# Forty projection heads and the block inverses of a DeltaNet layer: order from a scheduler, or from a list in the kernel

## The chip, the cores and the metric

The kernel runs on one core of a Trainium2 chip. The metric is the device time of one launch in microseconds; three runs of the kernel before took 1217.75, 1218.33 and 1227.18 us, the median is 1218.33 us. The profile is of a further execution. Engines are named as in the profile: PE (matmul), PEld (its weight loads), DVE, ACT, POOL, and SP, which here only issues transfers.

## The reference, cut to what matters

Two layers work on 512 latent tokens and 256 context tokens of width 1024, in float32. Layer 0 is a bidirectional gated DeltaNet, layer 1 is attention. The change is in layer 0 alone:

```python
p = u @ w_in                                    # 1024 -> 8192 + 64
qkv = silu(centred_dwconv(p[..., :4096], conv_w))   # five taps per channel
z = p[..., 4096:6144]
q, k, v = split(qkv)        # 8 heads of q, 8 of k, 16 of v, each of 128
...
decay = exp(where(lower, gc[..., :, None] - gc[..., None, :], -inf))
a = where(strict, einsum('cd,sd->cs', kb, kc) * decay, 0)
t_inv = triangular_solve(eye + a, eye)          # per chunk of 64, per head, per direction
qk = einsum('cd,sd->cs', qc, kc) * decay
...
o, s = scan over the chunks with t_inv, qk, k, q, v, in both directions
y = (rms_norm(o) * silu(z)) @ w_out
```

## The kernel before, in words

All 768 tokens lie as 6 tiles of 128 (NT = 6); a tile pairs a chunk of 64 that the forward scan visits with the chunk that the backward scan visits at the same time. Products are float32 made of three passes: an operand is split into a rounded part (wh, uh) and a rest (wl, ul), and wh·uh, wh·ul and wl·uh add up in one PSUM bank.

The program has five stages: conditioning and the transposed input (uh, ul); the projection of 8 key heads (`k_head`); the projection of 8 query heads, 16 gate heads and 16 value heads, beside which the block inverses are made; the scan over the chunks; output projection and the attention layer. The change is in the third stage, from 166.9 to 601.9 us of the profile.

One of its 40 heads is: a 512 KB load of 128 weight columns (SP, tile w, 2 buffers), the rounding to wh (ACT) and the rest wl (DVE; for query heads POOL; 3 buffers each), 24 matmuls of 512 columns into one PSUM bank and 24 of 256 into another (`gemm_T`, L349; 4 banks in all, tag g), and what follows. For query and value heads that is the centre tap (ACT, L368), four taps (DVE, L371), a tanh that is written back into the bank (ACT, L374) and the product that makes SiLU (DVE, L376 or L382), which frees the bank. Query heads are then squared and summed by PE (L504) and stored (q_d); value heads are turned by PE (`to_tokens`, L397), copied by ACT (L768) and stored (v_d) from ACT's queue. Gate heads need only tanh and one product (L778, L779) and a store (z_d).

The block inverses of tile t are made of 32x32 blocks. `t_masked` loads keys (kk) and two sheets of decay rows (df, each 4 broadcast transfers of 128 KB), takes Gram matrices on PE (G, L604), masks them, turns each df into decays by 16 small activations and one exponential (ACT, `decay_of`), and multiplies: md, and mo in four products of 32 partitions each. md is turned (DVE) and weighted (POOL) into L. `t_solve` solves two tiles at a time by columns on POOL (31 pairs of instructions, L682 and L683). `t_join` turns the inverse (U, DVE), takes two sets of 64 block products on PE (pp, L704, and pw, L716) with a negation on ACT between (pn), copies all into Tt (ACT, L708 and L719) and stores t_d. `t_queries` makes the masked products of queries and keys (qk_d) in the same way; their product with df is on POOL.

What sets the order: `pieces` is a generator that yields after each of these parts. The loop over the heads takes them in the order q x8, z x5, (v v z) x8, z z z, splits the weights three heads ahead (`split_ahead`), and after a query, gate or value head takes 1, 3 or 2 parts, which may not be issued before that head's last matmul and the SiLU of the head before (`issue_after`). Within these limits a scheduler of the tile framework, which simulates the program when it is built, places each instruction in its engine's queue. Each engine runs its queue in order. The scan's first loads (`load_step`: cT, cv, cQK, ckt, then ck and cq of the next step) come from the same SP queue.

Of the kernel before, what the change touches and what calls it, by code (L numbers as in the profile page):

```python
# [86 lines left out]
def backbone(tc, a, out):  # L87
# [56 lines left out]
    ul = up.tile([P, KT, NTOK], F32R, tag="ul", name="ul")  # L144

# [176 lines left out]
    split_at = [None, None]  # L322

    def load_w(src, c0, m, nm, E=V):
# [5 lines left out]
        split_at[1] = S.copy(wh[:, :, :m], w[:, :, :m]).ins  # L330
        split_at[0] = E.tensor_tensor(wl[:, :, :m], w[:, :, :m], wh[:, :, :m], ALU.subtract).ins  # L331
        return wh, wl

    tails, at, done = [], [0, None], []

    def turn_tails(age):

        while tails and tails[0][0] <= at[0] - age:
            with tc.issue_after(at[1]):
                tails.pop(0)[1]()  # L340

    def gemm_T(wh, wl, m, nm):

        out_ = []
        for c0, n in ((NCTX, NLAT), (0, NCTX)):
            pg_ = pa.tile([P, 512], F32, tag="g", name=f"g{n}_{nm}", bufs=4)
            for k in range(KT):
                for n_, (w, u) in enumerate(((wh, uh), (wh, ul), (wl, uh))):
                    mm = T.matmul(pg_[:m, :n], w[:, k, :m], u[:, k, c0:c0 + n], start=k == 0 and n_ == 0, stop=k == KT - 1 and n_ == 2)  # L349
            out_.append(pg_)  # L350
            at[1] = mm.ins
            turn_tails(2)
        return out_[1], out_[0]

    split = {}

    def split_ahead(ct, nm, E):

        split[ct] = load_w(w_in, ct * P, P, nm, E)

    def conv_silu(ct, nm, E=V, pool=None, bufs=2, swap=None):

        wh, wl = split.pop(ct) if ct in split else load_w(w_in, ct * P, P, nm, E)
# [9 lines left out]
        for ps, c0, n in ((p5, NCTX, NLAT), (p2, 0, NCTX)):  # L373
            e0 = S.activation(ps[:, :n], acc[:, c0:c0 + n], AF.Tanh)  # L374
            if swap is None:
                e1 = V.scalar_tensor_tensor(s[:, c0:c0 + n], ps[:, :n], 1.0, acc[:, c0:c0 + n], ALU.add, ALU.mult)  # L376
                continue
            h_ = n // 2
            for a0, o0, st_ in ((0, swap * 64, P), (h_, n - P + 64 - swap * 64, -P)):
                dst = raw(s, c0 + o0, [[st_, h_ // 64], [1, 64]])  # L380
                src = [y.rearrange("p (c r) -> p c r", r=64) for y in (ps[:, a0:a0 + h_], acc[:, c0 + a0:c0 + a0 + h_])]
                e1 = V.scalar_tensor_tensor(dst, src[0], 1.0, src[1], ALU.add, ALU.mult)  # L382
        done.append((e0.ins, e1.ins))
# [102 lines left out]
    for b in range(4):  # L486
        for v in range(2):
            r0 = b * 32 + v * 16
            dma(bball[r0:r0 + 16], be_d[v ^ (b // 2)].rearrange("t h c -> h t c")[:, :, b * 32:b * 32 + 32])
# [41 lines left out]
    def q_head(hh):  # L531
# [269 lines left out]
    for _ in work:  # L801
        pass
# [1013 lines left out]
```

## Time and profile before

| | |
|---|---|
| median of 3 runs | 1218.33 us |
| the profiled execution | 1220.96 us, its span 1219.2 us |
| PE busy in the span | 1144.4 us, 94% |
| DVE, ACT, POOL busy | 800.2, 731.5, 579.1 us |
| third stage | 166.9 to 601.9 us |
| mean granted clock of PE in the span | 0.978 |

The span runs from the first to the last instruction on the core; launch and end lie around it (1.8 us here). Matmuls are pipelined and their ends are modelled, so that PE's busy time over many matmuls says when it had work, not how fast it went; how fast is read from the distance between the starts. Busy times of other engines can be added.

### The profile page before, as it was taken

What the parts mean: (1) busy time and instruction counts of PE and PEld (TensorE: products, weight loads), DVE (VectorE), ACT (ScalarE), POOL (GpSimd) and SP (SyncE); (2) the same over time, 40 slices, a digit from 0 to 9 for tenths busy, and PEclk for the clock granted to TensorE, in tenths of its full rate; (3) what the DMA queues carried; (4) which work ended last, traced back from release to release, by engine and by line L of the source; (5) the groups of instructions that cost most, each with busy time, mean ns of one, the idle gap of its engine ahead of it and who ended that gap; (6) DMA issues with size and microseconds to landing.
All of it is one profiled execution on the core that took longest, in us unless ns stands there. A gap on an engine that the chain in (4) does not pass through costs nothing. (4 is left out here: it accounts for less than half of the span.)

```text
span 1219.2 us, 27757 instructions
## 1 busy us (share of the span) xinstructions
PE 1144.4 (94%) x10739; PEld 928.9 (76%) x10739; DVE 800.2 (66%) x1734; ACT 731.5 (60%) x1945; POOL 579.1 (47%) x442
## 2 busy tenths in 40 slices
PE   4999999999789989899999999899999999999996
PEld 1677678888678877788856666688887889999884
DVE  2688565777879645675478888635556566566646
ACT  3344336675565678896268999686663236666731
POOL 0131114229999999830067568455753344230810
PEclk9999899999899998899999999999999999999998
DMA  9465986454436569752999999266672202101323
GB/s 335 137 227 169 338 258 191 130 166 155 132 111 178 162 187 280 235 177 98 295 267 242 260 270 250 76 223 190 217 233 98 70 26 80 52 19 53 104 69 87
DMA packets 171125, 208.73 MB, mean 171 GB/s; under 512 B 12497, under 2 KB 126322, under 8 KB 170226
## 3 DMA queue, kind: packets, MB, share of 16 engines
q1 hardware_dynamic: 151346, 197.02, 53.8%
q10 hardware_dynamic: 19648, 9.94, 2.9%
q8 instruction: 85, 1.39, 0.5%
q14 instruction: 46, 0.38, 0.1%
HBM read 166.16 MB, written 40.67 MB: 170 GB/s over the span
## 5 line engine op out<-in xcount | busy, mean ns | idle before, releaser
L918 POOL TENSOR_TENSOR S<-S,glb 128x512 f32<-128x512 f32 x80 | 81.7, 1043 | 122.0 <-PE ks L909 122.0
L1076 PE MATMUL po<-woh,y 128*128 128x512 f32 x384 | 130.0, 403 | 0.7 <-ACT y L1052 0.7
L349 PE MATMUL g_v<-uh,wh 128*128 128x512 f32 (+1 forms) x256 | 91.4, 357 | 14.8 <-DVE sil_v L376 14.8
L1025 POOL TENSOR_TENSOR wol<-wo,woh 128x1024 fp32r<-128x1024 f32 x32 | 77.1, 2411 | 55.6 <-ACT woh L1018 52.7
L683 POOL TENSOR_TENSOR X<-X,tmp 128x62 f32<-128x62 f32 (+15 forms) x93 | 95.8, 1031 | 6.5
L371 DVE SCALAR_TENSOR_TENSOR acc_v<-g_v,cwv,acc_v 128x510 f32<-128x510 f32 (+3 forms) x128 | 74.5, 610 | 33.9 <-ACT acc_v L368 32.3
L349 PE MATMUL g_z<-uh,wh 128*128 128x512 f32 (+1 forms) x256 | 88.6, 346 | 5.7 <-DVE sil_v L376 5.7
L682 POOL TENSOR_TENSOR tmp<-L,X 128x62 f32<-128x62 f32 (+15 forms) x93 | 89.0, 957 | 6.9
L349 PE MATMUL g_v<-ul,wh 128*128 128x512 f32 (+1 forms) x256 | 89.6, 350 | 0.0
L349 PE MATMUL g_v<-uh,wl 128*128 128x512 f32 (+1 forms) x256 | 88.7, 346 | 0.0
L349 PE MATMUL g_z<-ul,wh 128*128 128x512 f32 (+1 forms) x256 | 87.3, 341 | 0.0
L349 PE MATMUL g_z<-uh,wl 128*128 128x512 f32 (+1 forms) x256 | 87.1, 340 | 0.0
L1076 PEld LDWEIGHTS po<-woh,y 128*128 128x128 f32 x384 | 72.5, 189 | 16.0 <-ACT y L1052 0.9
L1076 PE MATMUL po<-wol,y 128*128 128x512 f32 x192 | 75.7, 395 | 0.9 <-POOL wol L1025 0.9
L349 PEld LDWEIGHTS g_v<-uh,wh 128*128 128x128 f32 x256 | 50.6, 198 | 21.6 <-DVE sil_v L376 15.5
L331 POOL TENSOR_TENSOR wl_k<-w_k,wh_k 128x1024 fp32r<-128x1024 f32 x8 | 19.3, 2415 | 94.6 <-ACT wh_k L330 94.6
L331 POOL TENSOR_TENSOR wl<-w,wh 128x1024 fp32r<-128x1024 f32 x8 | 19.4, 2426 | 83.6 <-ACT wh L330 83.6
L349 PEld LDWEIGHTS g_z<-uh,wh 128*128 128x128 f32 x256 | 49.2, 192 | 11.6 <-DVE sil_v L376 6.4
L331 DVE TENSOR_TENSOR wl<-w,wh 128x1024 fp32r<-128x1024 f32 x32 | 49.9, 1560 | 11.6 <-ACT wh L330 11.6
L1050 DVE SCALAR_TENSOR_TENSOR pt<-pt,og,z 128x128 f32<-128x128 f32 x96 | 34.4, 358 | 34.7 <-PE pt L1041 31.9
L909 PE MATMUL ks<-S,ck 128*64 128x256 f32 x352 | 55.2, 392 | 0.4 <-ACT o L915 0.4
L983 DVE TENSOR_TENSOR S<-su,S 128x512 f32<-128x512 f32 x80 | 51.5, 686 | 6.0 <-PE su L969 3.9
(375 smaller groups left out, 3397.4 us busy)
## 6 DMA issues: line engine op xcount, KB each, us to landing
aw<-in_ada_w SPq DMA_DIRECT2D x24, 1024.0 KB, 7.3
w<-in_dn_w_in SPq DMA_DIRECT2D x40, 512.0 KB, 4.6
wo<-in_dn_w_out SPq DMA_DIRECT2D x32, 512.0 KB, 3.3
cv<-v_d SPq DMA_DIRECT2D x48, 256.0 KB, 8.0
df<-gc_d SPq DMA_DIRECT2D x48, 128.0 KB, 2.8
z_d<-zs SPq DMA_DIRECT2D x16, 384.0 KB, 5.8
v_d<-vt ACTq DMA_DIRECT2D x16, 384.0 KB, 4.0
t_d<-Tt SPq DMA_DIRECT2D x6, 1024.0 KB, 5.1
```

Source lines behind the costliest of these rows:

```text
L331: split_at[0] = E.tensor_tensor(wl[:, :, :m], w[:, :, :m], wh[:, :, :m], ALU.subtract).ins
L349: mm = T.matmul(pg_[:m, :n], w[:, k, :m], u[:, k, c0:c0 + n], start=k == 0 and n_ == 0, stop=k == KT - 1 and n_ == 2)
L371: V.scalar_tensor_tensor(acc[:, c0 + lo:c0 + hi], ps[:, lo + j - 2:hi + j - 2], cwv[:, j, ct:ct + 1], acc[:, c0 + lo:c0 + hi], ALU.mult, A ...
L682: E.tensor_tensor(tv, bcast(L[:, :, j + 1:, j], 3, j + 1), bcast(X[:, :, j, 0:j + 1], 2, n), ALU.mult)
L683: E.tensor_tensor(X[:, :, j + 1:, 0:j + 1], X[:, :, j + 1:, 0:j + 1], tv, ALU.subtract)
L909: T.matmul(ks[r0:r0 + 64, w], kq[w][:, hh, r0:r0 + 64], St[hh][:, d], start=True, stop=True)
L918: G.tensor_tensor(St[hh], St[hh], bcast(g_, 3, P), ALU.mult)
L983: V.tensor_tensor(St[hh], sj, St[hh], ALU.add)
L1025: G.tensor_tensor(wl, raws.pop(n), halves[n][0], ALU.subtract)
L1050: V.scalar_tensor_tensor(pj, pj, og, raw(z, off, [[st_, 2], [1, 64]]), ALU.mult, ALU.mult)
L1076: T.matmul(acc[:, nh], y[i][:, j, :], ww[k][:, nh * 512:(nh + 1) * 512], start=h == 0 and x == 0, stop=h == VH - 1 and x == 2)
```

## The change

The generators, `split_ahead`, `issue_after` and the loop over the heads are gone. All work of the third stage is written as some 750 pieces, each with an engine, a cost in microseconds, a due time, the pieces that it must follow, the buffers that it takes and holds and, for a transfer, a time to land. A greedy pass (`written_out`) goes through them when the program is built: it takes the piece that could start first by these costs, and among equals the one with the earlier due time. The order so found is fixed for all five engines (`manual_schedule`). The costs serve only for the order.

The order of heads becomes z q x8, then v v z x8. A head's bank work is cut into its two parts (512 and 256 columns). The rest wl of query heads moves from POOL to DVE. The weights of a head may be loaded as soon as a buffer is free. The numbers of buffers change: 4 for df in place of 2 (and a borrowed md), Tt has one in place of two. The decay rows are laid out by `lane`, so that all blocks of mo come from the first of the two sheets; mo becomes one product of 128 partitions. The scan and everything behind it are the same.

```diff
+    def lane(b, d):
+        return d ^ (1 - b % 2)
...
+    gcM = ap_.tile(W6, F32, tag="gcM", name="gcM", bufs=1)
+    for b in range(4):
+        for v in range(2):
+            V.tensor_copy(gcM[b * 32:b * 32 + 32, v], gc[b * 32:b * 32 + 32, lane(b, v)])
...
-                decayed(V, md[:, v], df[:, :, 0:32], Gx[:, :, 0:32])
-                for b in ((1, 2), (0, 3))[v]:
-                    r = slice(b * 32, b * 32 + 32)
-                    decayed(V, mo[r], df[r, :, 32:64], Gx[r, :, 32:64])
+        decayed(V, mds[t][:, v], df[:, :, 0:32], Gx[:, :, 0:32])
+        if v == 0:
+            decayed(V, mos[t], df[:, :, 32:64], Gx[:, :, 32:64])
...
-    order = "z" * 5 + "vvz" * 8 + "zzz"
-    heads = [(q_head, h) for h in range(QH)]
...
-        f_(h)
-        with tc.issue_after(split_at[0]), tc.issue_after(split_at[1]), tc.issue_after(at[1]), tc.issue_after(done[-2][0]), tc.issue_after(done[-2][1]):
-            for _ in range({q_head: 1, z_head: 3, v_head: 2}[f_]):
-                next(work, None)
+    order = "zqzqzqzqzqzqzqzqvvzvvzvvzvvzvvzvvzvvzvvz"
...
+    def ready_at(x):
+        at = x.since
+        for y in x.after:
+            if y.end is None:
+                return None
+            at = max(at, y.end + (y.lands if y.engine != x.engine or y.engine == "SP" else 0.0))
...
+        return at + margin(x)
...
+    for n, (c, h) in enumerate(heads):
+        t0 = n * SLOT
+        w = kept(("w", n), Piece("SP", 0.4, t0 - 30, w_load, n, takes=["w"], lands=6.0, since=-99.0))
+        wh = kept(("wh", n), Piece("ACT", 1.05, t0 - 9, w_high, n, after=[w], takes=["wh"], holds=[("w", w)], lands=0.1))
+        G_ = n in ()
+        wl = Piece("POOL" if G_ else "DVE", 2.4 if G_ else 1.5, t0 - 5, w_low, n, G if G_ else V, after=[wh], holds=[("w", w)], lands=0.1)
+        g = []
+        for i in range(2):
+            g.append(Piece("PE", (5.5, 2.9)[i], t0, gemm_part, n, i, after=[wh, wl] + ([last["g", n - 1]] if n and not i else g), takes=["g"], holds=[("wh", wh)], lands=0.2))
...
+    written_p = tc.manual_schedule(engines={T.engine, V.engine, S.engine, G.engine, nc.sync.engine})
+    written_p.__enter__()
+    for _, x in written_out():
+        x.fn()
+    written_p.__exit__(None, None, None)
```

Two places of the program show what moves. The first is the start of the stage. SP's queue before, where the last key head's store (kt7) is issued; w_4 and w_5 are the weights of the fifth and sixth query head:

```order
L329 DMA w_4_2016<-in_dn_w_in 128x8x128
L241 DMA gate_d1_79<-gt100_1603 128x512
L235 DMA gb11_1748<-in_ada_b 128x512
L519 DMA kt_d_65<-kt7_1717 128x6x128
L329 DMA w_5_2138<-in_dn_w_in 128x8x128
L241 DMA gate_d1_79<-gt101_1752 128x512
```

and the same place of SP's queue now; w_z1 and w_q1 are the weights of the third and fourth head of the stage, df0_0m and df1_0m the decay rows of tile 0:

```order
L505 DMA kt_d_65<-kt7_1726 128x6x128
L245 DMA gate_d1_79<-gt101_1761 128x512
L553 DMA df0_0m_1779<-gc_d_69 32x1024 x4
L553 DMA df1_0m_1784<-gc_d_69 32x1024 x4
L723 DMA w_z1_1803<-in_dn_w_in 128x8x128
L723 DMA w_q1_1836<-in_dn_w_in 128x8x128
```

Before, the weights of five heads are asked for ahead of the stores of the last key head; now those of two are, and the third head's come behind these stores and behind the first decay rows. ACT's queue at that place, before; wh_4 is the rounding for the fifth head, and df0_0 are the decays of tile 0:

```order
L526 COPY kb7_1721<-kb1_7_1728 128x2x2x64
L368 ACTIVATE acc_q1_1942<-g512_q1_1892,cwv_74 128x512
L529 DMA k_d_63<-kb7_1721 128x6x128
L534 COPY rq_94<-ss_q0_1857 128x6
L330 CAST wh_4_2017<-w_4_2016 128x1024
```

and now, where the rounding for the third head, wh_z1, stands behind the first sheet of decays:

```order
L515 DMA k_d_63<-kb7_1730 128x6x128
L566 ACTIVATE df0_0m_1779<-df0_0m_1779,gcM_513 128x64 x16
L568 ACTIVATE df0_0m_1779<-df0_0m_1779 128x1024
L566 ACTIVATE df1_0m_1784<-df1_0m_1784,gcM_513 128x64 x6
L765 ACTIVATE sil_z0_1879<-g512_z0_1805 128x512
L728 CAST wh_z1_1881<-w_z1_1803 128x1024
```

ACT now takes 23 instructions on the decays and one on the first gate head before it rounds the weights of the third head. The second place is the end of the stage. SP's queue before; t_d is written from Tt0 and Tt1, elX, cT_0, cv_0, cQK_0 and ckt_0 are the loads of the scan's first step, ck_1 of its second:

```order
L720 DMA t_d_71<-Tt1_1760 128x2048
L781 DMA z_d_68<-zs12_6858 128x768
L850 DMA elX_7097<-elV_90 64x192 x2
L873 DMA cT_0_7106<-t_d_71 128x1024
L878 DMA cv_0_7107<-v_d0_66 64x1024 x2
L881 DMA cQK_0_7108<-qk_d_72 128x4x128
L883 DMA cQK_0_7108<-qk_d_72 64x4x128 x2
L884 DMA ckt_0_7109<-kt_d_65 128x1024
L872 DMA ck_1_7214<-k_d_63 128x1024
L872 DMA cq_1_7215<-q_d_64 128x1024
L781 DMA z_d_68<-zs13_6932 128x768
```

and now:

```order
L815 DMA z_d_68<-sil_z14_6518 128x768
L670 DMA t_d_71<-Tt_1768 128x2048
L815 DMA z_d_68<-sil_z15_6948 128x768
L670 DMA t_d_71<-Tt_1768 128x2048
L1036 DMA elX_7080<-elV_90 64x192 x2
L1059 DMA cT_0_7089<-t_d_71 128x1024
L1064 DMA cv_0_7090<-v_d0_66 64x1024 x2
L1064 DMA cv_0_7090<-v_d1_67 64x1024 x2
L1067 DMA cQK_0_7091<-qk_d_72 128x4x128
L1069 DMA cQK_0_7091<-qk_d_72 64x4x128 x2
L1070 DMA ckt_0_7092<-kt_d_65 128x1024
```

Before, the loads of the scan's first step stand ahead of the stores of the last three gate heads; now all of them stand behind the store of the last gate head (z15) and behind the last store of t_d. On PE the last head's matmuls are now followed by pp and pw of tile 5 and the turn of value head 15, and then by the scan's first product; before, pp and pw of tile 5 and all turns stood ahead of the last two or more gate heads.

More of the change, by code (lines that the diff above doesn't have):

```diff
@@ L800, in backbone, with q_gram @@
[L800 to L805 removed]
+    def q_gram(t):
+        grams[t] = []
+        for gq, kq in enumerate(kks.pop(t)):
+            ps = pa.tile([P, 4, P], F32, tag="gq", name=f"GQ{gq}_{t}")
+            for h4 in range(4):
+                for hf in range(2):
+                    r0 = hf * 64
+                    T.matmul(ps[r0:r0 + 64, h4, 0:64], kq[:, 0, h4, r0:r0 + 64], kq[:, 1, h4, r0:r0 + 64], start=True, stop=True)
+            grams[t].append(ps)
@@ new lines, in head_squared, with head_summed @@
+    def head_squared(n):
+        sums[n] = ap_.tile([P, NT, P], F32, tag="tok", name=f"sq_q{heads[n][1]}").rearrange("p t k -> p (t k)")
+        S.activation(sums[n], sils[n], AF.Square)
+    def head_summed(n):
+        ps = turns[n] = pa.tile([P, 512], F32, tag="tr", name=f"ss_q{heads[n][1]}")
+        sq = sums.pop(n)
+        for t in range(NT):
+            for hf in range(2):
+                c0 = t * P + hf * 64
+                T.matmul(ps[hf * 64:hf * 64 + 64, t:t + 1], sq[:, c0:c0 + 64], ones, start=True, stop=True)
```

550 lines of the change are left out of this document (330 added, 220 removed).

## The prediction

> **What bounds the kernel now.** I read the page first. The busy line shows PE at work nearly all the time, the clock line next to full:
>
> ```profile
> PE 1144.4 (94%) x10739; PEld 928.9 (76%) x10739; DVE 800.2 (66%) x1734; ACT 731.5 (60%) x1945; POOL 579.1 (47%) x442
> PEclk9999899999899998899999999999999999999998
> ```
>
> But the change is in the third stage alone, so I cut windows: first the stage, then one undisturbed head, then stretches around gaps, last the scan's first 36 us.
>
> ```profile
> core 0: us, PE busy (x) PEld busy (x) DVE busy (x) ACT busy (x) POOL busy (x), PEclk, DMA share, GB/s
> 166.91:601.92 435.01, 406.01 (x4392) 350.27 (x4390) 292.39 (x443) 283.75 (x720) 266.88 (x230) 0.97 0.60 180
> 192.52:200.86 8.34, 8.34 (x50) 7.38 (x49) 3.33 (x9) 4.18 (x12) 3.44 (x4) 1.00 0.81 201
> 321.17:331.46 10.29, 3.10 (x27) 2.90 (x25) 9.99 (x14) 4.65 (x9) 9.74 (x8) 0.85 0.44 130
> 331.46:338.81 7.35, 7.35 (x25) 5.94 (x25) 4.16 (x6) 6.00 (x20) 6.80 (x8) 0.74 0.47 141
> 459.78:467.76 7.98, 7.98 (x24) 6.33 (x25) 6.52 (x12) 6.87 (x22) 7.67 (x6) 0.67 0.95 274
> 506.60:515.05 8.45, 8.45 (x25) 6.65 (x26) 6.87 (x8) 7.58 (x22) 5.50 (x5) 0.63 0.77 241
> 604.00:640.00 36.00, 32.67 (x548) 21.16 (x544) 26.07 (x68) 22.66 (x65) 18.97 (x18) 1.00 1.02 265
> ```
>
> PE is busy 406.0 of the stage's 435.0 us; the next engine, DVE, 292.4. So PE bounds the stage on average, and 29.0 us are idle. The fourth row shows what an idle stretch is: PE works 3.1 of 10.3 us while DVE works 10.0. The rows behind it show what follows: 24 matmuls of 512 columns, 5.47 us in the head of 192.52 (the other 2.87 are its 256 columns), take 7.35 to 8.45 at clocks of 0.74 to 0.63. The waits of the stage name the cause:
>
> ```profile
> PE g_v L349 <- DVE sil_v L376: 14.8, 4, 7.2
> PE g_z L349 <- DVE sil_v L376: 5.7, 4, 3.5
> ```
>
> PE stands because DVE reaches the SiLU that frees a bank too late. The chain of waits covers only the last of the program and says nothing here.
>
> **The floor of the stage.** Forty heads at 8.34 us are 333.6. The other products of PE:
>
> ```profile
> L397 PE MATMUL tr_v<-ident,sil_v 128*128 128x128 f32 x96 | 13.9, 275 | 1.8 <-DVE sil_v L376 1.8
> L704 PE MATMUL pp<-U,mo 32*32 32x32 f32 x768 | 8.5, 193 | 0.0
> L716 PE MATMUL pw<-pn,U 32*32 32x32 f32 x768 | 7.8, 193 | 2.1 <-ACT pn L710 2.1
> L604 PE MATMUL G<-kk 128*32 128x64 f32 x384 | 7.2, 221 | 0.0
> L504 PE MATMUL ss_q<-ones,sq_q 128*64 128x1 f32 x192 | 6.9, 199 | 0.0
> L653 PE MATMUL GQ1q<-kq1q 128*64 128x64 f32 x96 | 4.2, 233 | 0.0
> L653 PE MATMUL GQ0q<-kq0q 128*64 128x64 f32 x96 | 4.1, 228 | 4.6 <-issue 4.6
> ```
>
> They are 52.6 us, with overlaps counted in; some 46 without, if all shrink as tile 5's pp does there (8.5 / 6 is 1.4 a tile, while one set takes 1.2 from first to last). So the rows give 380, without the last key heads' small products. From above, 435.0 less 29.0 idle and less 13 for the clock (0.97 of 435) gives 393. I take 388, nearer the upper figure since the lower leaves groups out. The stage holds 47 us over its floor.
>
> **What the change removes.** The 47 us are, by these rows, waits for DVE and the slow clock behind them. In the order z q the bank-freeing work of DVE alternates between gate heads, with one product a bank, and query heads, with four taps and a SiLU; and the parts of the inverses no longer come in lumps after a head. I count all 47 as gone, and then charge every new wait by itself. DVE has room: mo's 24 small products become 6, the size of md (both 512 elements long per partition). The weights' rests of the queries move the other way, to DVE:
>
> ```profile
> L331 DVE TENSOR_TENSOR wl<-w,wh x32: 1215/1336/3310, 231.7 to 580.6; 128x1024 fp32r<-128x1024 f32 x32
> L562 DVE TENSOR_TENSOR mo<-df,Gx x24: 672/1337/1720, 214.6 to 375.2; 32x512 f32<-32x512 f32 x24
> L562 DVE TENSOR_TENSOR md<-df,Gx x12: 675/733/1384, 212.5 to 372.3; 128x512 f32<-128x512 f32 x12
> ```
>
> mo loses 24 x 1.17 - 6 x 0.93 = 22 us (mean durations; the shortest mo and the shortest md agree, 672 and 675 ns, so full width costs no more), wl adds 8 x 1.56 = 12.5, gcM eight small copies. DVE comes to about 285 of 388 us, ACT stays near 284, POOL loses about 20. None becomes the bound by its sum, which hides these edits; if that cover went, all 12.5 of wl would show.
>
> **What it adds: the early wait.** The third head's weights now stand in SP's queue behind gate_d, and behind eight df issues; its rounding stands on ACT behind 22 small decays, an exponential and a tanh. The rows of these steps:
>
> ```profile
> w<-in_dn_w_in SPq DMA_DIRECT2D x40, 512.0 KB, 4.6
> 186.38 0.34 SPq L241 DMA_DIRECT2D gate_d<-gt  x1
> 193.59 3.67 SPq L575 DMA_DIRECT2D df<-gc_d  x8
> 198.98 3.70 ACT L581 ACTIVATE df<-df,gcV 128x64 f32<-128x64 f32 x15 [1.72 <-DMA df<-gc_d]
> 204.14 1.04 ACT L330 CAST wh<-w 128x1024 fp32r<-128x1024 f32 x1
> L778 ACT ACTIVATE zs<-g_z 128x512 f32<-128x512 f32 (+1 forms) x32 | 15.4, 487 | 20.3 <-PE g_z L349 14.2 <-DMA z_d<-zs 5.0 <-ACT g_q L374 0.6
> ```
>
> Decays began 5.4 us after the first df issue (198.98 - 193.59). From 186.7: decays start at 192.1, 16 of 0.25 end at 196.1, the exponential (1.05, as long as wh) at 197.2, six more at 198.7, the tanh of a gate head (487 ns) at 199.2, wh 1.04 at 200.3, wl (median 1336 ns) at 201.6. Before, the third head begins at 192.52; the first two are as long in the new order, less one query's sums, so PE is free at about 191. The wait is some 10.5 us. The rows of 0.74 to 0.63 show 2 to 3 us of slow clock behind a gap (7.98 - 5.47), so 2.5 more, and 1 for tile 0's Gram products that fall in it. That is 14. Lower bound 4: with decays and weights in PE's shadow if the DMA lands them sooner; upper bound 18, if the following head meets the same. I take 14, since every step has its own row. The weights alone would land at 191.3 + 4.6 and be ready at 198.3, 7.5 us late. The Trainium skill ("TensorE: Matmul & The Clock Gate", specification table) says ScalarE's queue is strictly first in, first out, by which the whole 10.5 stands and not 7.5. The rows above agree: wh at 204.14 runs after the decays that stand ahead of it.
>
> Smaller waits from an order fixed by estimated costs: 5 us, between 0 and 12; the nearest rows are the wait of pw for pn (2.1 in 3 waits) and tr_v's (1.8).
>
> **What it adds: the end of the stage.** Before, the scan follows the last head without a gap, because its loads were asked for 20 us ahead:
>
> ```profile
> 580.84 2.35 SPq L850 DMA_DIRECT2D elX<-elV  x2
> 583.24 0.59 SPq L873 DMA_DIRECT2D cT<-t_d  x1
> 583.93 1.98 SPq L878 DMA_DIRECT2D cv<-v_d  x2
> 601.92 0.67 PE L935 MATMUL pr<-cv,cT 64*64 64x128 f32 x16
> v_d<-vt ACTq DMA_DIRECT2D x16, 384.0 KB, 4.0
> t_d<-Tt SPq DMA_DIRECT2D x6, 1024.0 KB, 5.1
> L719 ACT COPY Tt<-pw 32x512 f32<-32x512 f32 x24 | 13.9, 578 | 0.7 <-PE pw L716 0.4
> L768 ACT COPY vt<-tr_v 128x512 f32<-128x512 f32 (+1 forms) x32 | 13.8, 477 | 3.7 <-PE tr_v L397 3.7
> ```
>
> Now pp and pw of tile 5 come after the last head's end E. pp takes 1.2, pw 1.2, pn between them about as much as a copy of 578 ns, 0.6; ACT's copies of the turned value head take 1.0, the four copies of pw 2.3. That is 6.3, with the steps from engine to engine some 7: t_d is issued at E + 7 and lands 5.1 later, and v_d of the last head lands at about the same time. Then come cT (0.5 MB), cv (4 x 0.25), cQK (0.5) and ckt (0.5). These 2.5 MB and t_d's 1 MB take 13 us at the 265 GB/s of the scan's window, so from E + 7 to E + 20. The products su, which need ckt, start there, where before they start 2.3 behind the last head (604.2, by the windows' 604). The end costs 18. The scan doesn't catch that up: PE is busy 32.7 of its first 36 us. Against it, the 3 us of pp, pw and the last turn are in the floor of 388 and now lie inside this gap, so 3 come off once. Bounds of the 18: 10, if loads that depend on neither t_d nor the last v_d are through by then; 22, if the store of z15 and the second step's loads share the queue.
>
> **The sum.** Removed 47, and 3 for products that now lie in the gap; added 14 early, 5 in small waits, 18 at the end: 50 - 37 = 13 us gained. The profiled execution took 1220.96 us with a span of 1219.2; the span becomes 1206. The median of the runs shown, 1218.33, lies 2.6 below that execution, so the forecast is 1205.
>
> **Rivals.**
>
> Both new waits mostly hidden: early wait 4, small waits 2, end 8. For it speaks that DMA is busy 0.60 of the stage, so room is there; against it the queue order. 50 - 4 - 2 - 8 = 36, about 1182. The block by POOL and the late DVE, below, keep the forecast's other terms.
>
> DVE's order costs more than it saves, and the result is slower. DVE takes the turns of U and of L and the wl of 40 heads in one fixed order; where one waits for a late producer, or starts just ahead of a SiLU, that SiLU frees its bank late:
>
> ```profile
> L698 DVE STREAM_TRANSPOSE U<-X 128x1024 f32<-128x1024 f32 x12 | 24.6, 2120 | 0.0
> ```
>  One such wait costs 14.8 / 4 = 3.7 and 1.9 of slow clock, 5.6 us. If 6 of the twelve turns do this, it is 34 us, of which 5 are counted: 13 - 29, about 1234. From six such places on it is slower by over 1%. For it speaks that waits of this kind are already the main idle time; against it that DVE is idle 140 us of the stage.
>
> DVE's wl blocked by POOL: the wl row's maximum of 3310 ns is 1.75 above its mean of 1560, and POOL now runs its pairs beside eight more of them. 8 x 1.75 = 14 us in front of PE takes the gain: 1219. For it speaks the spread of 1215 to 3310; against it that the median is 1336, so most are undisturbed. The Trainium skill ("SBUF — State Buffer", "Who interferes with whom") says a DVE instruction with two SBUF inputs and a GpSimd instruction that reads SBUF exclude each other for a whole instruction. The spread agrees with that; no row tells which POOL instruction was in the way.
>
> **Chances.** The forecast (1192 to 1216 alone) 0.50, the hidden waits 0.20, the block by POOL 0.13, the late DVE 0.17. The range takes in the hidden waits (1182, and 1180 with their bound) and slower places up to 1232. One per cent, 12 us, is about what a measurement of this kernel can tell from no change: below 1206 is faster, above 1230.5 slower. The forecast falls below 1206 in 0.30 of its 0.50, which with 0.20 makes faster 0.50; the rest with the block by POOL makes same 0.33; slower is 0.17.
>
> **What would show it.** In the changed profile the last head ends at about 166.9 + 388 - 3 + 14 + 5 = 571, where before it ends at 601.9, and the first su starts near 591. The early wait shows as a PE wait of about 10 us near 191 for wl of z_1 with wh behind decays on ACT; if it is under 5, this step is wrong. The waits for DVE's SiLU, 20.5 us before, should be under 5. The end shows as a gap of 10 to 20 us between the last g product and the scan's su, waiting for DMA of cT, cv or ckt. DVE's mo should show 6 products of about 0.9 us. Slow places would show as windows at clocks of 0.6 to 0.75 in mid-stage; more than four of them, and the prediction is wrong upward. If ckt lands by E + 10, it is wrong downward.

## The result, and the profile after

The changed kernel takes 1225.66 us (median of 20 runs, 1218.19 to 1232.32) against 1219.24 for the kernel before in the same 20 rounds: a ratio of 1.0052, interval 1.0032 to 1.0072. It is slower by half a per cent, within 1%; the forecast was 1205. The profiled execution of the changed kernel is the longest of its 20, 1232.32 us with a span of 1230.5, so that where a size matters the other profiles with the same end stand beside it.

The page's busy and clock lines of the changed kernel look like those of before, with one low digit that was not there, in the twentieth slice (585 to 615 us):

```profile
PE 1145.7 (93%) x10739; PEld 927.6 (75%) x10739; DVE 800.8 (65%) x1732; ACT 733.3 (60%) x1945; POOL 559.3 (45%) x430
PEclk9999898999999999999589999999999999999998
```

The windows of the changed kernel: the stage from the first head to the last; then the gap at the start, the head behind it, the middle of the stage, the gap at the end and the scan's start.

```profile
core 0: us, PE busy (x) PEld busy (x) DVE busy (x) ACT busy (x) POOL busy (x), PEclk, DMA share, GB/s
170.55:578.33 407.78, 391.30 (x4123) 339.56 (x4121) 288.82 (x428) 277.31 (x707) 249.40 (x216) 0.98 0.60 180
191.06:203.20 12.14, 3.04 (x25) 2.83 (x24) 0.71 (x2) 7.88 (x26) 0.00 (x0) 0.73 1.06 257
203.20:213.53 10.33, 7.62 (x25) 5.39 (x25) 6.25 (x8) 10.30 (x34) 0.00 (x0) 0.82 0.78 221
217.00:578.33 361.33, 356.67 (x3869) 312.28 (x3868) 272.15 (x394) 251.40 (x632) 249.40 (x216) 1.00 0.58 177
578.33:597.53 19.20, 4.72 (x263) 4.06 (x263) 1.36 (x3) 7.86 (x15) 0.00 (x0) 0.60 0.63 175
597.53:640.00 42.47, 35.03 (x492) 22.56 (x496) 21.53 (x59) 18.67 (x53) 13.60 (x13) 0.78 1.09 240
```

And the same middle in the kernel before, to its last head:

```profile
217.00:601.92 384.92, 355.92 (x3993) 309.67 (x3991) 261.86 (x373) 254.67 (x651) 247.94 (x214) 0.96 0.58 177
```

In the middle the change does what its plan says: PE is idle for 4.7 us of 361.3 at full clock, where before it was idle for 29.0 of 384.9 at 0.96. The last head ends at 578.3, 23.6 us earlier. What is lost lies on both sides of it. PE's waits from 160 to 610 us name the places:

```profile
PE pr L1121 <- DMA cv<-v_d: 12.9, 2, 12.4
PE g_z L742 <- ACT wh_z L728: 9.1, 1, 9.1
PE g_v L742 <- DVE sil_v L776: 3.5, 2, 2.1
PE G L580 <- DMA kq_0m<-k_d: 2.7, 1, 2.7
PE pq L1147 <- DMA cQK<-qk_d: 2.2, 2, 1.4
...
PE g_z L742 <- DVE sil_v L776: 1.1, 1, 1.1
```

The waits for DVE's SiLU, 20.5 us before, are 4.6. In their place stand one wait for wh_z at the start and one for the scan's data. (The name behind an arrow is what came last: wh_z is the rounding on ACT of a gate head's weights, kq the keys of a tile for the Gram products G.) SP's and ACT's timeline of the changed kernel at the start:

```profile
189.40 5.05 SPq L553 DMA_DIRECT2D df_0m<-gc_d  x8
194.54 0.40 SPq L723 DMA_DIRECT2D w_z<-in_dn_w_in  x1
...
195.29 3.92 ACT L566 ACTIVATE df_0m<-df_0m,gcM 128x64 f32<-128x64 f32 x16 [5.68 <-DMA df_0m<-gc_d]
202.12 1.03 ACT L728 CAST wh_z<-w_z 128x1024 fp32r<-128x1024 f32 x1
```

The third head's weights are asked for behind eight df issues, and rounded behind the decays, at 202.12; PE has been free since 194. And at the end, SP's queue, then PE:

```profile
583.60 0.32 SPq L815 DMA_DIRECT2D z_d<-sil_z  x1
586.04 0.32 SPq L670 DMA_DIRECT2D t_d<-Tt  x1
586.41 1.92 SPq L1036 DMA_DIRECT2D elX<-elV  x2
588.43 1.39 SPq L1059 DMA_DIRECT2D cT<-t_d  x1
589.91 3.19 SPq L1064 DMA_DIRECT2D cv<-v_d  x4
596.26 0.32 SPq L1070 DMA_DIRECT2D ckt<-kt_d  x1
...
578.33 1.29 PE L655 MATMUL pp<-U,mo 32*32 32x32 f32 x128
597.53 0.65 PE L1121 MATMUL pr<-cv,cT 64*64 64x128 f32 x2 [12.42 <-DMA cv<-v_d]
605.70 0.70 PE L1155 MATMUL su<-vd,ckt 64*64 64x256 f32 x4
```

The scan's loads begin at 586.41, which is 5.6 us later than before (580.84), though the last head ends 23.6 us earlier. The first su comes 27.4 us behind the last head, where before it came 2.3 behind it. That leaves the two kernels 1.5 us apart at this point (604.22 and 605.70). Then the scan itself falls back. It has 22 half-steps of 32 su products, and from the sixth on both kernels run at 7.55 us each; here is the start of each half-step's first su in the traces:

| half-step | before | changed | difference |
|---|---|---|---|
| 0 | 604.22 | 605.70 | 1.5 |
| 1 | 611.70 | 613.29 | 1.6 |
| 2 | 620.04 | 626.80 | 6.8 |
| 4 | 636.82 | 646.82 | 10.0 |
| 5 | 644.56 | 656.05 | 11.5 |
| 10 | 682.31 | 693.80 | 11.5 |

Five half-steps take 40.3 us before and 50.4 in this execution; nothing behind them differs, and 11.3 us are the whole difference of the spans.

### The profile page after: what moved, and what is told of

It is laid out like the page before. It is cut to its first block, busy times and chain, and to the rows that moved or that the text cites. A ratio compares the mean times of both kernels' runs of the same rounds, so it can differ in the third digit from the quotient of the medians.

```text
span 1230.5 us, 27673 instructions
## 1 busy us (share of the span) xinstructions
PE 1145.7 (93%) x10739; PEld 927.6 (75%) x10739; DVE 800.8 (65%) x1732; ACT 733.3 (60%) x1945; POOL 559.3 (45%) x430
## 5 line engine op out<-in xcount | busy, mean ns | idle before, releaser
L1211 POOL TENSOR_TENSOR wol<-wo,woh 128x1024 fp32r<-128x1024 f32 x32 | 77.1, 2412 | 55.6 <-ACT woh L1204 52.6
L742 PE MATMUL g_z<-uh,wh_z 128*128 128x512 f32 (+1 forms) x256 | 88.9, 347 | 10.2 <-ACT wh_z L728 9.1
L742 PE MATMUL g_v<-uh,wh_v 128*128 128x512 f32 (+1 forms) x256 | 87.9, 343 | 3.5 <-DVE sil_v L776 3.5
L742 PE MATMUL g_z<-uh,wl_z 128*128 128x512 f32 (+1 forms) x256 | 87.4, 341 | 0.0
L742 PE MATMUL g_z<-ul,wh_z 128*128 128x512 f32 (+1 forms) x256 | 87.1, 340 | 0.0
L742 PE MATMUL g_v<-ul,wh_v 128*128 128x512 f32 (+1 forms) x256 | 86.1, 337 | 0.0
L742 PE MATMUL g_v<-uh,wl_v 128*128 128x512 f32 (+1 forms) x256 | 86.1, 336 | 0.0
L1262 PEld LDWEIGHTS po<-woh,y 128*128 128x128 f32 x384 | 72.5, 189 | 15.9 <-ACT y L1238 0.9
L615 POOL TENSOR_TENSOR L<-L,bball 128x1024 f32<-128x1024 f32 x6 | 13.2, 2193 | 133.0 <-DMA z_d<-sil_z 112.2
L742 PEld LDWEIGHTS g_z<-uh,wh_z 128*128 128x128 f32 x256 | 49.3, 192 | 16.2 <-ACT wh_z L728 9.3
L1098 DVE SCALAR_TENSOR_TENSOR r<-ks,negV,cv 128x128 f32<-128x128 f32 x176 | 52.1, 344 | 6.2 <-DMA cv<-v_d 4.2
L742 PEld LDWEIGHTS g_v<-uh,wh_v 128*128 128x128 f32 x256 | 48.6, 190 | 9.2 <-DVE sil_v L776 3.9
```

Source lines behind the costliest of these rows:

```text
L742: T.matmul(ps[:, :m], w[:, k], u[:, k, c0:c0 + m], start=k == 0 and n_ == 0, stop=k == KT - 1 and n_ == 2)
L1098: V.scalar_tensor_tensor(r[:, 2 * j + i], ks[:, 0, i], negV[:, visit, t, h:h + 1], v[:, h], ALU.mult, ALU.add)
L1211: G.tensor_tensor(wl, raws.pop(n), halves[n][0], ALU.subtract)
L1262: T.matmul(acc[:, nh], y[i][:, j, :], ww[k][:, nh * 512:(nh + 1) * 512], start=h == 0 and x == 0, stop=h == VH - 1 and x == 2)
```

## The experiments

Where nothing else is named, "less" and "more" are against the changed kernel's median of 1225.66 us, and the ratio in brackets is to the kernel before in the rounds of the experiment. That kernel's median moved with the rounds, from 1217.22 us beside x1 to x4 to 1219.54, so the ratios give differences that are up to 2.3 us other than the medians: against the changed kernel's 1.0052, x1 is 9.1 less and not 11.4, x4 3.4 more and not 1.2, z2 2.7 more and not 1.5. No reading below rests on 2 us.

**x1: the weights ahead of the decay rows.** One number in the list:

```diff
-            row_loads.append(Piece("SP", 2.0 - queries, due, decay_rows, t, v, not queries, takes=["df"], lands=4.0, after=row_loads[-1:]))
+            row_loads.append(Piece("SP", 2.0 - queries, due, decay_rows, t, v, not queries, takes=["df"], lands=4.0, since=16.0, after=row_loads[-1:]))
```

> The changed kernel with the first decay rows held back by one number in the list, so that the third and fourth head's weights stand ahead of them in SP's queue and their roundings ahead of the decays on ACT. My theory (the end: the scan's loads start only when SP has passed the last stores of t_d and z, and these hang on the solves of POOL): the 9.1 us wait of PE for wh_z near 194 goes and the last head ends 10 to 16 us before the changed kernel's 578.4, but the loads start at most 6 us earlier, so that the time falls by 0 to 7 us, to 1219 to 1226. Rival (the early wait is the whole miss): 13 to 16 us less, 1210 to 1213.

Measured: 1214.24 us, 11.4 less (ratio to the kernel before 0.9977, 0.9947 to 1.0007). The wait for wh_z is gone and the last head ends at 562.3, 16.1 us earlier. My half of the expectation was wrong: the loads come earlier by as much. The time lies between the two ranges, nearer to the rival's. Rows of x1, POOL's end and SP's first scan load:

```profile
506.63 5.73 POOL L633 TENSOR_TENSOR X<-X,bball 128x1024 f32<-128x1024 f32 x2
...
571.68 1.39 SPq L1059 DMA_DIRECT2D cT<-t_d  x1
```

and POOL's same instruction in the changed kernel:

```profile
522.35 5.75 POOL L633 TENSOR_TENSOR X<-X,bball 128x1024 f32<-128x1024 f32 x2
```

The solves end 15.7 us earlier too, and cT is issued 16.8 us earlier (588.43 in the changed kernel). So the start's delay goes through the whole stage, joins included, and the gap at the end stays: su still follows the last head by 25.2 us (587.5 - 562.3).

**x2: the end of the change, put into the kernel before.** The scan's loads are held behind the last gate head's store:

```diff
-        dma(z_d[h], s[:, 0:NTOK])
+        last_z[0] = dma(z_d[h], s[:, 0:NTOK]).ins
...
+        with tc.issue_after(last_z[0]):
             for hf in range(2):
                 dma(elX[hf * 64:hf * 64 + 64], elV[64 - hf * 64:128 - hf * 64])
...
             if p == 0:
-                load_step(s)
+                with tc.issue_after(last_z[0]):
+                    load_step(s)
```

> The kernel before with one thing of the change alone: the scan's first loads are issued only behind the store of the last gate head. My theory: the last head still ends near 602, but the first su follows it by 20 to 30 us in place of 2.3, and the time grows by 18 to 28 us, to 1237 to 1247. Rival (the scan has slack, or its loads are quick enough): at most 8 us more, under 1228.

Measured: 1239.11 us (1.0166, 1.0132 to 1.0200), 21.9 more than the kernel before in the same rounds (1217.22). Rows of x2:

```profile
580.88 22.78 SPq L781 DMA_DIRECT2D z_d<-zs  x4
603.75 1.14 SPq L852 DMA_DIRECT2D elX<-elV  x2
...
611.35 0.66 PE L938 MATMUL pr<-cv,cT 64*64 64x128 f32 x2 [8.91 <-DMA cv<-v_d]
618.93 1.56 PE L972 MATMUL su<-vd,ckt 64*64 64x256 f32 x12
```

The last head ends at 602.4 as before; su follows it by 16.5 us, and the five half-steps behind it take 45.4 in place of 40.3. Late loads alone cost the kernel before 14.7 us up to the first su and 5.1 in the half-steps. The time is in the range that I gave; the 16.5 are under the 20 to 30. This shows the cause without any other part of the change.

**x3: the joins earlier.** Same heads; POOL's solves aren't broken by products of the queries any more, and the last gate's store is left to the scheduler:

```diff
-    MARGIN = {"PE": 3.0, "ACT": 0.5, "DVE": 0.5, "POOL": 0.3}
+    MARGIN = {"PE": 1.0, "ACT": 0.5, "DVE": 0.5, "POOL": 0.0}
...
-        else:
+        elif c == "q" or h < 16 - 1:
             kept(("stored", c, h), Piece("SP", 0.6, e + 14, head_stored, n, after=si, holds=[("sil", sq_[0])], lands=6.0))
...
-        k, r = keys_and_rows(t, True, due - 12, after=[last["stored", "q", h] for h in range(QH)])
+        k, r = keys_and_rows(t, True, due - 12, since=due - 4, after=[last["stored", "q", h] for h in range(QH)])
...
-            G_ = t < 6
+            G_ = t < 2
...
     written_p.__exit__(None, None, None)
+    for n in range(N - 1, N):
+        head_stored(n)
```

(One more edit, here and in all later orders, lets a head's second tanh follow its first.)

> The changed kernel with the same order of heads and another end: POOL's solves follow one another without the products of the queries in between (four tiles of these go to DVE), PE takes join products 1 us and not 3 us after they are ready, and the last gate head's store is left out of the list. So the last store of t_d and with it the scan's first loads come well before the last head ends. My theory: loads start 20 us or more before the last head's end, the first su comes within 10 us of it, the 9 us wait at the start stays, and the time is 18 to 28 us under the changed kernel's: 1198 to 1208. Rival (the loss at the end is the clock's or the scan's own): su is 20 us or more behind the last head as now, 1220 to 1230.

Measured: 1212.50 us (0.9946, 0.9926 to 0.9965), 13.2 less, above the range that I gave. The end is as expected. In rows of x3, the last t_d, the loads, and the waits that are new:

```profile
544.87 0.32 SPq L670 DMA_DIRECT2D t_d<-Tt  x1
545.73 2.17 SPq L1038 DMA_DIRECT2D elX<-elV  x2
...
PE g_z L742 <- DVE sil_v L776: 5.2, 1, 5.2
PE pr L1123 <- DMA cv<-v_d: 4.9, 2, 4.2
PE g_v L742 <- issue: 4.8, 2, 3.1
```

The loads go out 40 us before the last head ends, and su follows it by 3.3 us in place of 27.4. But that head ends at 585.8, 7.4 later. DVE has more to do (318.7 us from 166.8 to 604, 295.3 in the changed kernel), yet that isn't what PE waits for: the 5.2 us for DVE's SiLU end at 397.3 and the longer of the two waits put down to issue at 357.3, while the first query product that was moved to DVE runs at 437.9. The order of DVE's other work has changed too; which part of it makes these waits, no run tells. And the first half-step takes 12.6 us in place of 7.5 (the five take 43.0): cv of the last value heads is issued only at 590.84, when their v_d, sent at 587.14, has landed. At the sixth half-step x3 is 24.0 us ahead of the changed kernel (632.07 and 656.05), but its span is only 17.0 shorter (1213.5 and 1230.5): the rest of the scan and what follows take 581.5 us in this profile, where the changed kernel and the kernel before take 574.5 and 574.6. In the other runs that rest is 573.7 to 580.0, and no run tells what it hangs on.

**x4: mo in four products again.**

```diff
-            decayed(V, mos[t], df[:, :, 32:64], Gx[:, :, 32:64])
+            for b in range(4):
+                r = slice(b * 32, b * 32 + 32)
+                decayed(V, mos[t][r], df[r, :, 32:64], Gx[r, :, 32:64])
```

> The changed kernel with the off-diagonal mask products undone: each of the six products of 128 partitions as four of 32 again, in the same order. My theory (DVE has slack): DVE's busy time grows by 15 to 22 us and the time by at most 3. Rival (DVE's queue sets when PE's banks come free): 8 us or more, over 1233, with new waits of PE for DVE's SiLU.

Measured: 1226.83 us (1.0080, 1.0048 to 1.0112), 1.2 more (3.4 by the ratio), far from the rival's 8. DVE's busy time from 166.8 to 604 us is 314.2 us against 295.3, 18.9 more. The full-width products save what they should on DVE, and that isn't where the time goes.

**y4: the old order of heads in the new list** (with x3's edit of `since` for the query keys and its small edit of the tanh).

```diff
-    order = "zqzqzqzqzqzqzqzqvvzvvzvvzvvzvvzvvzvvzvvz"
+    order = "qqqqqqqqzzzzzvvzvvzvvzvvzvvzvvzvvzvvzzzz"
```

> The changed kernel with the kernel before's order of heads (eight queries, five gates, then value and gate heads), everything else by the list. Theory (the pieces and not the alternation of gate and query heads took the waits for DVE's SiLU away): these waits stay under 8 us in the stage; with heavy query heads first the joins end later, and the time is 1226 to 1240. Rival (the alternation took them away): 15 us of such waits or more, as before, and over 1240.

Measured: 1235.83 us (1.0148, 1.0115 to 1.0180). PE's waits for DVE's SiLU in y4:

```profile
PE g_q L742 <- DVE sil_q L782: 16.1, 1, 16.1
...
PE g_z L742 <- DVE sil_v L776: 7.0, 2, 6.1
```

The 16.1 us lie from 191 to 207, where a query head's SiLU is late at the stage's start; the rest of the stage has 7.0, where the kernel before has 20.5. The time is in my range, but the waits are 23.1 in all, the rival's "15 us or more"; my "under 8" holds only without the first, which the kernel before doesn't have. The pieces take away most of the waits in the middle with either order of heads; what the order of heads changes is the wait at the start (16.1 here, 9.1 for wh_z in the changed kernel).

**z2: the queries' rests back on POOL** (`G_ = n in ()` becomes `G_ = c == "q"`).

> The changed kernel with the rests wl of the eight query heads back on POOL, everything else by the list. Theory (they cost nothing on DVE, and POOL's solves set the end of the joins): DVE's busy time in the stage falls by about 10 us, POOL's grows by about 19, and the time moves by less than 4 us. Rival (wl on DVE is in PE's way, by the port that it shares with POOL or by the queue): 8 us or more faster.

Measured: 1227.21 us (1.0074, 1.0035 to 1.0113), 1.5 more than the changed kernel. DVE's busy time falls by 8.2 us (287.1 from 166.8 to 604), POOL's grows by 11.2 (some 19 were expected). It makes no difference that can be told.

**z1 and z4: fewer loads in the scan's first steps.** In z1 cq and ckt of steps 1 to 5 are left out and ck serves for both:

```diff
-                for w, src in enumerate((k_d, q_d)):
+                for w, src in enumerate((k_d, q_d)[:1 if s < 6 else 2]):
                     dma(kq[w], src[t])
+                if s < 6:
+                    kq[1] = kq[0]
...
-            mark[0] = dma(kt, kt_d[t]).ins
+            if 0 < s < 6:
+                kt = kq[0]
+            else:
+                mark[0] = dma(kt, kt_d[t]).ins
```

> The changed kernel, with part of the scan's loads left out: in the steps 1 to 5 cq and ckt aren't loaded and ck stands for both, so that about 1 of 3.5 MB a step is missing and the output is another. Theory (behind a late start the first five steps go at the pace of their loads): from the first su of step 0 to that of step 5 it takes 38 to 42 us in place of 50.4 (37.7 at the scan's later pace), and the time falls by 5 to 11 us, to 1215 to 1221. Rival (the slow clock behind the gap, or ACT and DVE at the scan's start): 46 us or more, within 3 us of the changed kernel.

Measured: 1225.36 us (1.0046, 1.0025 to 1.0066), and 45.0 us for the five half-steps: the time is the rival's, the half-steps are in neither range. The trace shows why it tells nothing: the free buffers let cq and ckt of later steps go out at once (605.97 to 608.01), in the middle of the stretch. So in z4 the tiles stay taken, filled by POOL:

```diff
                 for w, src in enumerate((k_d, q_d)):
-                    dma(kq[w], src[t])
+                    if w and s < 4:
+                        G.memset(kq[w], 0.01)
+                    else:
+                        dma(kq[w], src[t])
...
-            mark[0] = dma(kt, kt_d[t]).ins
+            if 0 < s < 4:
+                G.memset(kt, 0.01)
+            else:
+                mark[0] = dma(kt, kt_d[t]).ins
```

> The changed kernel, with cq and ckt of the scan's steps 1 to 3 not loaded but filled with a constant by POOL, so that 1 MB of 3.5 a step is missing there, the buffers stay taken and no later load moves into the room (in the run z1 the later loads of cq and ckt could); the output is another. Theory (the slow first steps wait for the volume of their loads): the first five half-steps, from the first su on, take 38 to 41 us, and the time is 5 to 9 us under the changed kernel's 1225.7. Rival (the slow clock behind the gap and the chain of a half-step itself): 44 us or more, and within 3 us of 1225.7.

Measured: 1219.59 us (0.9994, 0.9974 to 1.0015), 6.1 less, and 39.7 us for the five half-steps (601.17 to 640.91). Both in the theory's range: behind a late start the first half-steps wait for the volume of their loads.

**y1, y2, y3, z3: both mends.** y1 is x1's edit and x3's together:

> The later decay rows of the run x1 and the early joins of the run x3 together, in the changed kernel's order of heads. If the wait at the start and the wait for the scan's loads are two separate costs, the gains add up: 1225.7 - 11.4 - 13.2 = 1201, so 1196 to 1206, without a wait for wh_z near 190 and with su within 10 us of the last head. Rival (both runs mended the same thing, the time at which the joins end): 1208 to 1214.

Measured: 1206.22 us (0.9904, 0.9872 to 0.9937), just above the range for a sum; most of both gains stays. As in x3, su comes 3.3 us behind the last head but the first half-step takes long (13.9 us), behind cv of the last value heads. y2 has another order of heads besides, with three gate heads last, whose stores are left to the scheduler (`h < 16 - 3`), POOL's margin as in the change, and earlier due times for the last joins:

```diff
-    order = "zqzqzqzqzqzqzqzqvvzvvzvvzvvzvvzvvzvvzvvz"
+    order = "zqzqqqqzzqqzqzvvzvvzvvvvzvvzzvvzvvzvvzzz"
-    MARGIN = {"PE": 3.0, "ACT": 0.5, "DVE": 0.5, "POOL": 0.3}
+    MARGIN = {"PE": 1.0, "ACT": 0.5, "DVE": 0.5, "POOL": 0.3}
...
-        due = (150, 160, 245, 255, 330, 340)[t]
+        due = (150, 160, 245, 255, 300, 310)[t]
```

> Both mends, with the heads in an order that ends in three gate heads, whose stores stand behind the scan's first loads, so that neither t_d nor the last value head's v_d is late for the scan. My theory (scan loads that start early enough cost nothing, and PE's floor is the rest): the last head ends at 555 to 570, the first su within 4 us of it, the first five steps lose under 5 us, and the time is 1178 to 1194, faster than both kernels. Rival (value heads in groups of four bring DVE's late SiLU back): waits of PE for DVE's SiLU over 15 us and 1200 or more.

Measured: 1194.78 us (0.9810, 0.9775 to 0.9844), just above the range, 1.9% faster than the kernel before and with z3 the fastest form. Rows of y2 at the end of the stage:

```profile
551.97 0.32 SPq L670 DMA_DIRECT2D t_d<-Tt  x1
554.01 2.25 SPq L1038 DMA_DIRECT2D elX<-elV  x2
...
569.88 0.67 PE L1123 MATMUL pr<-cv,cT 64*64 64x128 f32 x16
572.18 1.04 PE L1157 MATMUL su<-vd,ckt 64*64 64x256 f32 x16
```

The scan's first product comes right behind the last head (570.0), as in the kernel before, 32 us earlier. The first five half-steps take 45.6 us, more than I expected (under 43); the scan's loads begin 16 us ahead, but of the second step's only ck and cq go out early; cT and what follows it go out from 570.8 on, behind the last cv of the first step (569.63), which had waited 5.0 us for v_d. In y3 the last join has buffers of its own (tags of the first solves for U and Tt of tile 5), the query products of three tiles and not two stay on POOL, and the heads go `zqzqzqqqqqzqzzzvvzvvvvzvvzvvzvzvvvzvvzzz`:

> As the run with three gate heads last, another such order, and the last tile's join in buffers of its own that the first solves have left free, so that it doesn't wait for the join ahead of it. My theory: the last t_d is stored 30 us or more before the last head ends, the time is 1176 to 1192. If the last join was no longer late in the run before it, the two are within 5 us of each other. Rival as there: 1200 or more.

Measured: 1197.79 us (0.9852, 0.9810 to 0.9893), no better, as the second sentence there allows. The last t_d goes out at 539.4, 27 us before the last head ends, so the loads' lead was there; the first half-step, behind cv of the last value heads, takes 15.9 us.

z3 is y2 with `since=max(12.0, due - 12)` for the first keys:

> The run y2 (three gates last) with the keys of the first tiles loaded up to 12 us earlier. Theory: PE's wait for kq of tile 0 (3.1 us there) goes, and the time falls by 2 to 5 us, to 1190 to 1193. Rival (the wait is off the path, or another transfer takes its place): within 1 us of y2's 1194.8.

Measured: 1194.05 us (0.9813, 0.9770 to 0.9857). PE's wait for kq of tile 0 is 5.4 us, where y2 has 3.1, and not 0: the rival, and no gain that can be told.

## Why the prediction was wrong

**What bounds the kernel, and the 47 us: right.** PE's floor was put at 388 us, 3 of which now lie behind the last head, so 385. From the first head to the last the changed kernel takes 407.8; without 15.7 at the start (28.0 us from 191.06 to 219.06 for 12.3 us of products) and the 5 us of small waits it is 387. (One sum of the floor was off by a microsecond: 52.6 shrunk as tile 5's pp does is 45 and not 46. Nothing hangs on it.) The waits for DVE went from 20.5 to 4.6, the clock of the middle from 0.96 to 1.00.

**The parts costed at nothing: right, as far as can be told.** Undone, the full-width products cost 1.2 us by the medians (x4) and the move of wl 1.5 (z2), 3.4 and 2.7 by the ratios; both intervals overlap that of the changed kernel. mo took 0.7 to 1.7 us in the changed kernel, 7.3 in all, 20.7 less where 22 was worked out:

```profile
L541 DVE TENSOR_TENSOR mo<-df_5m,Gx 128x512 f32<-128x512 f32 x1 | 1.7, 1678 | 0.0
...
L541 DVE TENSOR_TENSOR mo<-df_1m,Gx 128x512 f32<-128x512 f32 x1 | 0.7, 684 | 0.0
```

**The early wait: right in mechanism, the size partly by luck.** 14 was forecast, with wh of the third head at 199 to 200; it ran at 202.1, PE lost 15.7, and taking it away gave 9 to 11. The wait itself is 9.1 of the 10.5 that were worked out. Another 2.7 are a wait that wasn't in the sum, of tile 0's Gram products for their keys (kq); the rest is the slow clock behind both (0.73 and 0.82 in the two windows). What each row said was late was late in that order. The Trainium skill ("TensorE: Matmul & The Clock Gate", specification table: ScalarE's queue is strictly first in, first out) agrees with this trace: wh, whose weights were asked for at 194.5, ran at 202.1 behind all of the decays that stood ahead of it. The start of the first head was 3.6 us later in this execution than before (170.55 and 166.91); in x1, x3 and x4 it began at 166.1 to 167.1, in z4 at 171.0, so that varies from profile to profile and isn't the change's.

**The end: the step that failed.** The prediction put 18 us on it: su at E + 20, E being the last head's end, and "the scan doesn't catch that up". Both halves were too small. First, su came at E + 27.4, and at E + 24.6 to 25.4 in the four other runs with this end (x4, z1, z2, z4). The issue of t_d was right (E + 7.7, forecast E + 7); the 13 us for the loads behind it were not:

```profile
586.04:604.51 18.47, 3.60 (x37) 2.06 (x37) 1.86 (x9) 2.03 (x4) 0.00 (x0) 0.50 1.01 229
...
604.51 1.12 PE L1147 MATMUL pq<-vn,cQK 64*64 64x128 f32 x12 [0.79 <-DMA cQK<-qk_d]
```

From the issue of t_d to the end of pq's wait for cQK the DMA engines are busy throughout (share 1.01) and move 4.2 MB (18.47 x 229) where the sum had 3.5 MB at 265 GB/s; the last head's v_d (384 KB) wasn't in it, nor the next step's loads, which start before the first step's have landed. I had let su wait for ckt alone. Ahead of it stand pr, the copy vn and pq, with data of their own: pr waited for cv until E + 19.2, pq for cQK until E + 26.2, and su follows 1.2 us behind. So the 8.2 us from pr to su, 2.3 before (601.92 to 604.22), are set by the landing of cQK, all but the last 1.2; PE's half clock (0.50 in this window) is paid in those. Second, the scan not only didn't catch up, it fell further back: its first five half-steps took 50.4 us (44.1 in z2, 46.7 in x4) against 40.3. Before, the first step's data lay ready, and the second's were on their way, 20 us ahead of the first product; without that lead the first half-steps wait for their loads, at a DMA share of 1.09 from 597 to 640 us. The wait that stretches the second half-step stands on DVE, and the scan's next products wait for it through ACT:

```profile
616.05 1.13 DVE L1098 SCALAR_TENSOR_TENSOR r<-ks,negV,cv 128x128 f32<-128x128 f32 x4 [4.22 <-DMA cv<-v_d]
```

z4 shows that it is their volume: with a part of these loads gone the half-steps take 39.7. I had read the row 604 to 640 of before (DMA share 1.02, 265 GB/s) for its rate and not for what it says: there is no DMA to spare behind a late start. So the term that I took as 18 is 27.4 - 2.3 + 10.0 = 35 in this profile and 26 in z2's (24.6 - 2.3 + 3.7). x2 measures it apart from everything else: 21.9 us in the kernel before.

By terms, for the profiled execution: the span came to 1230.5 where 1206.2 was forecast, 24.3 more: 3.6 for the start of that execution, 3.8 for the rest before the last head's end (578.3 and 570.9), 7.4 up to su, 10.0 in the half-steps, and -0.5 in roundings and behind them. Against the median of the runs the miss is 20.7. That 1225.66 lies inside the range that I gave is no merit of the sum: the range's upper part was there for slow places of DVE in mid-stage, and these cost 4.6 us.

**How it came to fail.** I priced the end from the last head on, as a chain behind it. What sets it is when the scan's loads go out, and that hangs on the last join and on the order of SP's queue, not on PE. (It hangs on the last value heads too: x3, y1 and y3 send the loads out 27 to 40 us ahead, and still their first half-steps take 12.6 to 15.9 us, behind cv.) They went out at 586.4 in the changed kernel and at 580.8 before: measured by the loads the stage had become longer, not shorter. The rows for this stood in the order of SP and in the start of elX; I used them for a price and not as the end of the stage.

**The rivals.** The hidden waits (1182) are refuted by the waits above. The late DVE (1234) has its place in the changed kernel, but at 4.6 us; it came back in number with the heads' old order (y4, 23.1). The wl blocked by POOL is real and off the path: PE's waits from 160 to 610 us in the changed kernel name no wl. The rows of wl in the changed kernel:

```profile
L731 DVE TENSOR_TENSOR wl_z<-w_z,wh_z 128x1024 fp32r<-128x1024 f32 x15 | 25.0, 1664 | 6.5 <-ACT wh_z L728 6.5
L731 DVE TENSOR_TENSOR wl_v<-w_v,wh_v 128x1024 fp32r<-128x1024 f32 x16 | 24.4, 1526 | 2.5 <-ACT wh_v L728 2.5
L731 DVE TENSOR_TENSOR wl_q<-w_q,wh_q 128x1024 fp32r<-128x1024 f32 x7 | 8.7, 1236 | 1.6 <-ACT wh_q L728 1.6
```

The seven on the queries, which the change moved, are the short ones. In the trace the ten of the stage's wl that have no POOL instruction beside them take 1214 to 1226 ns, and all that take over 1300 run beside POOL, the longest 2.9 us. Nine more run beside POOL and take no more than 1226. Two examples show what parts them: the wl at 481.42 takes 1.22 us, and POOL's product that begins 0.01 us behind it takes 2.36; the wl at 353.11, begun 0.12 us behind a product on POOL, takes 2.03. The Trainium skill ("SBUF — State Buffer", "Who interferes with whom") says that such a pair excludes each other for a whole instruction; the trace agrees in these rows. z2 moved only the short ones, so it can't price the others; that they cost little is read from PE's waits.

**What stays open.** The windows of the five half-steps, first in the kernel before and then in the changed one:

```profile
604.22:644.56 40.34, 37.02 (x632) 24.17 (x628) 29.55 (x75) 26.26 (x77) 23.07 (x22) 1.00 1.01 266
```

```profile
605.70:656.05 50.35, 42.98 (x624) 27.41 (x628) 28.79 (x70) 25.90 (x76) 23.12 (x22) 0.86 1.04 236
```

and in z2:

```profile
603.70:647.78 44.08, 39.09 (x624) 25.27 (x628) 30.24 (x70) 25.55 (x76) 23.10 (x22) 0.95 1.06 266
```

By rate and length the stretch moves 10.7 MB in the kernel before, 11.9 in the changed one and 11.7 in z2: behind a late start some 1 MB more has to land in it. At z2's 266 GB/s that is the 3.7 us by which z2's half-steps are longer than before. The other 6 us of this execution go with its lower rate; why the same loads move 236 GB/s here and 266 in z2, at nearly the same DMA share, no run tells.

The slow clock (0.86 over the changed kernel's half-steps, where it is at half up to 609.6 and again from 616.4 to 623.3) isn't needed for the loss: y2 has a full clock throughout and takes 45.6. And the runs x1, x4, z1 and z2, at clocks of 0.93 to 0.95, take 44.1 to 46.8, while z4 at 0.94 takes 39.7, so that at an equal clock 4 to 7 us are the loads'. How much of the 6 us is the clock's stays open.

## What to carry to other kernels

A stage ends where the next stage's loads can start, not where its last matmul ends: find the first load of the next stage in the queue, see what stands ahead of it, and cost the change by that time. Where the next stage runs at the rate of its loads, as the scan does here, a late start isn't paid once but again in its first steps until the buffers are ahead; read the DMA share of its first steps before calling a handover a fixed price. And a planner's list that begins at time 0 doesn't know what the stage ahead has left in the queues; its first instructions are the ones to check against the trace.

## What the runs showed of the hardware

Not expected: PE's clock stayed at half from 582.3 to 609.6 us, though PE worked 8.6 of the last 12.1 us of that time, in pieces between waits; this chain paid the clock as well as the waits. And a DVE product of two SBUF inputs of 128x1024 took 1.22 us alone and up to 2.9 beside POOL, 1.2 where it began ahead of POOL's instruction.
